# Six products into a residual, token-major instead of feature-major, in a two-block transformer kernel

## The chip, the core and the metric

The kernel runs on one core of a Trainium2 chip. The metric is the device time of one execution, in microseconds. Its engines, each with an instruction queue of its own: TensorE (PE, matmul), VectorE (DVE), ScalarE (ACT), GpSimd (POOL), SyncE (SP, which issues DMAs).

## The reference

Two blocks, of two layers each, over 256 latent tokens of width 1024 (the first block also carries 256 context tokens). Cut to what the change touches:

```
# first block, layer 1 (latents only)
h = h + ml[2] * (mix @ gdn_w_out)                                   # "dout"
h = h + ml[5] * (square(relu(modulate(rms_norm(h), ...) @ mlp_w1)) @ mlp_w2)   # "w2_1"
x = rms_norm(h, final_norm)
# second block, for l in (0, 1)
h = h + rms_norm(mixed @ w_out[l], norm_mix_post[l])                # "out0", "out1"
f = swiglu_ffn(rms_norm(h, norm_ffn_pre[l]), w_ffn_in[l], w_ffn_out[l])        # "fo0", "fo1"
h = h + rms_norm(f, norm_ffn_post[l])
```

All products are float32 in and out. `w_out` is 1024 x 1024, `mlp_w2` 4096 x 1024, `w_ffn_out` 2816 x 1024. Between the two layers of the second block the keys and values that layer 1 shares are made from the new h; the keys and values of a memory of 256 tokens are needed by both layers.

## The kernel before

The residual h lies feature-major: eight tiles of 128 features (partitions) x 256 tokens. A float32 product is three matmuls: both operands are split into a high part in the matmul's type and the remainder (hi and lo), and hi*hi, hi*lo and lo*hi are added up in PSUM. `load_w` fetches a weight tile of 128 x 1024 (512 KB) and splits it: ACT casts `whi` (L310), VectorE, or POOL where it is told to, subtracts for `wlo` (L311).

A product is feature-major: `gemm_fm` (L335 to L337) keeps 128x128 of the weights stationary and moves 256 tokens, for each of eight output tiles all its k tiles one after the other. `side_by_side` (L362 to L364) runs several output tiles k tile by k tile as activations arrive; most stretches begin with it, so L362 marks the first product behind a norm.

The norm's sum of squares of a token runs over the features, which are partitions. ACT squares each finished tile (L415, L418), POOL or VectorE adds the squares up (L419) while the next tile's product runs, TensorE adds the partitions with a column of ones (L398), VectorE takes x ** -0.5 by a polynomial (`newton`, L383 to L389: eight small dependent operations), and TensorE spreads the result over partitions (L408). In `post_norm` the norm falls on the product, so a copy of it, `mx`, waits for the factor: L1718 scales, L1719 adds to h, on VectorE for three tiles and on POOL for five. `fold` (L315, L316) then makes hi and lo of h times a weight for the next product, whose row factor is applied later, and `squares` (L1649, L1652) makes the next norm's squares.

Two lists of small work fill gaps: `fillers`, called by `fill`, and `sides`, called by `side`. In this part of the program the first holds `memory_prep` (memory tiles in hi and lo, with their norm), the second `memory_kv` (24 matmuls of 256 columns a step, with `mah`, `mal` for the memory, L335 to L337 or L345 to L347).

PSUM has two pools of four banks, `mm` and `sm`. The FFN (`ffn`) and the MLP (`mlp`) first make hidden tiles and then the output product; the MLP in four quarters of the hidden width, each adding to h (L759). The order of the engines' queues is set by a scheduler that works from the code's dependencies, the order the code calls in, and the pools.

Of the kernel before, what the change touches and what calls it, by code (L numbers as in the profile page):

```python
# [11 lines left out]
ALU = mybir.AluOpType  # L12
# [7 lines left out]
# x ** -0.5 = y * (p + P0) * (q + Q0) for a seed y with x * y * y within 0.93 .. 1.07, to 2.3e-8 of it  # L20
# [5 lines left out]
# ---------------------------------------------------------------- host layout  # L26
# [153 lines left out]
def _chunks_tm(w):  # L180
    """256 columns by half of K per block, for token-major products: [(N / 256) * 2, 128, 1024]"""
# [5 lines left out]
def host_arrays(i):  # L187
# [40 lines left out]
    ar["dout"] = _chunks(i["gdn_w_out"][0])  # L228
    for l in range(2):
# [3 lines left out]
        w = _chunks(i["w_ffn_out_2"][l])  # L233
        ar[f"fo{l}"] = np.ascontiguousarray(np.pad(w, ((0, 0), (0, 0), (0, 256))).reshape(8, 128, 3, 1024).transpose(0, 2, 1, 3))
# [6 lines left out]
    ar["out0"] = _chunks(i["w_out_2"][0])  # L241
    ar["out1"] = _chunks(i["w_out_2"][1][cat(order + [768 + al(256)])])
# [3 lines left out]
# ---------------------------------------------------------------- the kernel  # L246
# [3 lines left out]
class Kern:  # L250
# [12 lines left out]
    # ---- tiles  # L263
# [34 lines left out]
    def ftiles(self, n, name, R, dt=F32):  # L298
        """n feature tiles of [128, R]; two share a unit when R is 256"""
# [8 lines left out]
    # ---- building blocks  # L308
# [4 lines left out]
    def split_scaled(self, src, col, hi, lo):  # L313
        """hi + lo = src * col (per partition)"""
# [97 lines left out]
    def sq_acc(self, acc, src, first, eng):  # L412
        """acc += src ** 2"""
# [7 lines left out]
    def sq_accs(self, accs, src, f, eng, s=slice(0, 256)):  # L421
        """squares of the eight tiles of a norm, the last one's apart; s: the columns of src"""
# [4 lines left out]
    # ------------------------------------------------------------ program  # L427
# [4 lines left out]
    def body(self, es):  # L432
# [44 lines left out]
        acc = self.residual_out("dout", mix, 1, 2, 256, fills=2)  # L477
# [3 lines left out]
        acc = self.mlp(1, ah, al, 256, side_at=None)  # L481
# [24 lines left out]
    def ada_first(self, crow):  # L506
        """the first layer's shift and scale for each half of the feature tiles: on the tensor engine, but for the second half's scale"""
# [40 lines left out]
    def ada_cols(self, ps, out, bias):  # L548
        """rows of modulation vectors -> out, a column per feature tile, plus bias"""
# [28 lines left out]
    def side(self, n):  # L578
        """n steps of work on the tensor engine that only later parts wait for, where it would idle"""
# [8 lines left out]
    def fill(self, n):  # L588
        """up to n steps of work that other parts leave room for"""
# [8 lines left out]
    def by_turns(self, gens, turns):  # L598
        """the steps of several generators; turns: whose each one is, over and over"""
# [10 lines left out]
    def drain(self, n):  # L610
        """run the first n fillers to their end"""
# [7 lines left out]
    # ---- keys and values of the memory, both layers of the second block  # L619
    def memory_prep(self):  # L620
        """the memory in hi and lo parts, a feature tile per step, and its norm's factors"""
# [12 lines left out]
        y = self.rstd_cols([acc], 1024)  # L634
# [1056 lines left out]
    def post_norm(self, name, kt, weights, a, w, last=False, sides=(0, 0, 0), first=None, folds=()):  # L1691
# [24 lines left out]
        for f in range(8):  # L1716
# [6 lines left out]
            if False:  # L1723
                accs += self.squares([f], accs)
# [340 lines left out]
```

## Time and profile before

| | us |
|---|---|
| median of 3 runs | 1845.78 (1845.67 to 1847.97) |
| span of the profiled execution | 1845.4 |
| TensorE busy | 1750.0 (95%) |
| VectorE busy | 1320.7 (72%) |
| ACT busy | 824.8 (45%) |
| POOL busy | 372.2 (20%) |

The median lies 0.4 us above the span of the profiled execution. A busy share is an average over all stages. TensorE's 95% says little of a wait of some microseconds between two products: such waits are found in the engine's instructions in order of time, where the bracket behind an instruction gives the idle time ahead of it and what ended that. The granted clock is given per stretch, 1.00 being 2.4 GHz.

### The profile page before, as it was taken

Reading aid. Unit: us, or ns where it says so; the run is one execution under the profiler, and the core shown is the slowest. Engines: PE = TensorE matmul, PEld = TensorE weight load, DVE = VectorE, ACT = ScalarE, POOL = GpSimd, SP = SyncE. Lnnn points to the kernel's source line nnn. Section 1 sums busy time; section 2 is a strip of 40 time slices with the busy share of each in tenths; the row PEclk is TensorE's granted clock in tenths of the full one; section 3 lists DMA queues with packets and bytes.
Section 4 is the critical chain, followed back from the end, with each engine's and each line's share of the span. In section 5 each row is a group of like instructions: output and inputs, shape, how many; then the busy total and the mean of one; then the engine's idle time right before and its main releaser. Section 6 shows DMA issues by size and latency. Waiting matters only on the chain.

```text
span 1845.4 us, 31121 instructions
## 1 busy us (share of the span) xinstructions
PE 1750.0 (95%) x12076; PEld 1572.7 (85%) x12076; DVE 1320.7 (72%) x2443; ACT 824.8 (45%) x1476; POOL 372.2 (20%) x427
## 2 busy tenths in 40 slices
PE   8999999999999999888998999988999999999997
PEld 2786567888888889778997999987899998889997
DVE  6996787797957547689657766688777657677754
ACT  4433642532232336543334644556454435554442
POOL 1231131210201021136303000122211024231111
PEclk9999999899999999898798999999899999999999
DMA  8581001365747522235202555542455553145552
GB/s 316 161 273 58 23 18 57 102 216 172 246 166 245 172 93 88 64 103 151 57 25 80 182 182 185 180 146 69 150 190 184 174 184 126 47 140 185 184 174 85
DMA packets 99755, 260.82 MB, mean 141 GB/s; under 512 B 33492, under 2 KB 35412, under 8 KB 99352
## 3 DMA queue, kind: packets, MB, share of 16 engines
q1 hardware_dynamic: 99032, 257.47, 43.2%
q8 instruction: 95, 1.56, 0.3%
q10 hardware_dynamic: 576, 1.37, 0.2%
q14 instruction: 52, 0.43, 0.1%
HBM read 254.61 MB, written 4.19 MB: 140 GB/s over the span
## 4 chain that ended last, share of the span: by engine, by line
PE 71%; DVE 9%; ACT 2%; POOL 2%; issue 1%; DMA 0%; SPq 0%; POOLq 0%; ACTq 0%; DVEq 0%
PE mm L335 19%; PE mm L336 19%; PE mm L337 19%; PE mm L362 1%; PE mm L364 1%; PE mm L363 1%; DVE W L1393 1%; PE mm L1541 1%; DVE wlo L311 1%; PE mm L1532 1%; PE mm L1561 1%; PE sm L398 1%; DVE pr L1391 1%; PE sm L1578 1%; PE sm L1579 1%
## 5 line engine op out<-in xcount | busy, mean ns | idle before, releaser
L310 ACT CAST whi<-wst 128x1024 fp32r<-128x1024 f32 (+3 forms) x389 | 392.3, 1012 | 533.4 <-PE mm L336 288.1
L311 DVE TENSOR_TENSOR wlo<-wst,whi 128x1024 fp32r<-128x1024 f32 (+3 forms) x370 | 447.7, 1213 | 176.2 <-ACT whi L310 173.1
L335 PE MATMUL mm<-ah,whi 128*128 128x256 f32 (+1 forms) x1648 | 512.4, 313 | 3.7 <-DVE gs L1487 2.1
L336 PE MATMUL mm<-al,whi 128*128 128x256 f32 (+1 forms) x1648 | 513.4, 312 | 0.0
L337 PE MATMUL mm<-ah,wlo 128*128 128x256 f32 (+1 forms) x1648 | 512.5, 311 | 0.7 <-DVE wlo L311 0.7
L335 PEld LDWEIGHTS mm<-ah,whi 128*128 128x128 f32 x1648 | 316.7, 193 | 21.4 <-DVE gs L1487 2.5
L337 PEld LDWEIGHTS mm<-ah,wlo 128*128 128x128 f32 x1648 | 316.8, 192 | 17.2 <-DVE wlo L311 1.3
L336 PEld LDWEIGHTS mm<-al,whi 128*128 128x128 f32 x1648 | 317.1, 193 | 16.5 <-issue 0.8
L573 DVE SCALAR_TENSOR_TENSOR tmp<-adaw,crow 128x1024 bf16<-128x1024 f32 x134 | 162.1, 1236 | 4.3 <-DMA adaw<-in_ada 4.2
L335 PE MATMUL mm<-hh,whi 128*128 128x256 f32 (+1 forms) x480 | 159.7, 333 | 0.0
L336 PE MATMUL mm<-hl,whi 128*128 128x256 f32 (+1 forms) x480 | 159.6, 332 | 0.0
L337 PE MATMUL mm<-hh,wlo 128*128 128x256 f32 (+1 forms) x480 | 159.6, 332 | 0.0
L419 POOL TENSOR_TENSOR acc<-acc,tmp 128x256 f32<-128x256 f32 x57 | 63.1, 1117 | 435.0 <-ACT tmp L418 434.4
L575 POOL TENSOR_TENSOR mod<-mod,vecs 128x2 f32<-128x2 f32 (+1 forms) x84 | 62.7, 746 | 379.8 <-DVE tmp L573 339.2
L335 PE MATMUL mm<-fh,whi 128*128 128x256 f32 x352 | 99.6, 283 | 0.0
L336 PE MATMUL mm<-fl,whi 128*128 128x256 f32 x352 | 99.6, 283 | 0.0
L337 PE MATMUL mm<-fh,wlo 128*128 128x256 f32 x352 | 99.6, 283 | 0.0
L336 PEld LDWEIGHTS mm<-hl,whi 128*128 128x128 f32 x480 | 91.2, 190 | 8.8
L337 PEld LDWEIGHTS mm<-hh,wlo 128*128 128x128 f32 x480 | 91.2, 190 | 8.8
L335 PEld LDWEIGHTS mm<-hh,whi 128*128 128x128 f32 x480 | 91.2, 190 | 8.7
L759 DVE SCALAR_TENSOR_TENSOR h<-mm,mod,h 128x256 f32<-128x256 f32 x88 | 42.0, 481 | 68.5 <-PE mm L337 59.7
L335 PE MATMUL mm<-mh,whi 128*128 128x256 f32 (+1 forms) x240 | 76.3, 324 | 0.5 <-ACT whi L310 0.3
(471 smaller groups left out, 3312.0 us busy)
## 6 DMA issues: line engine op xcount, KB each, us to landing
wst<-in_w SPq DMA_DIRECT2D x128, 512.0 KB, 3.7
wst<-in_fin SPq DMA_DIRECT2D x88, 512.0 KB, 3.4
adaw<-in_ada SPq DMA_DIRECT2D x84, 512.0 KB, 4.3
wst<-in_fo SPq DMA_DIRECT2D x32, 512.0 KB, 3.4
wst<-in_dw SPq DMA_DIRECT2D x25, 512.0 KB, 3.3
wst<-in_out SPq DMA_DIRECT2D x16, 512.0 KB, 3.6
wst<-in_ew SPq DMA_DIRECT2D x14, 512.0 KB, 4.1
wst<-in_wa SPq DMA_DIRECT2D x14, 512.0 KB, 3.8
```

Source lines behind the costliest of these rows:

```text
L310: self.A.copy(hi, src)
L311: (lo_eng or self.V).tensor_tensor(lo, src, hi, ALU.subtract)
L335: T.matmul(out, lhsT=w[0][:, s], rhs=ah[k], start=(first and k == 0), stop=False)
L336: T.matmul(out, lhsT=w[0][:, s], rhs=al[k], start=False, stop=False)
L337: T.matmul(out, lhsT=w[1][:, s], rhs=ah[k], start=False, stop=(last and k == kt - 1))
L362: self.T.matmul(ps, lhsT=hi[:, s], rhs=ah[k], start=first and n == 0 and not (paired and i % 2), stop=False)
L363: self.T.matmul(ps, lhsT=lo[:, s], rhs=ah[k], start=False, stop=False)
L364: self.T.matmul(ps, lhsT=hi[:, s], rhs=al[k], start=False, stop=end)
L419: eng.tensor_tensor(acc, acc, s, ALU.add)
L573: V.scalar_tensor_tensor(self.tmp().bitcast(BF16), w, 0.5, crow[:, b], ALU.mult, ALU.mult, accum_out=m[:, b:b + 1])
L575: G.tensor_tensor(mm, mm, self.vec(f"adab{l}")[:, n:n + 1].to_broadcast([128, len(conds)]), ALU.add)
L759: self.V.scalar_tensor_tensor(h, ps[:, s], gt[:, f, b:b + 1], h, ALU.mult, ALU.add)
```

## The change

The six products become token-major, in a new class `Rows`. The activations are stationary (128 features of one k tile x 128 tokens), the weights move, 512 columns of a k tile's row block at a time. Four PSUM banks of the `sm` pool hold the result: two blocks of 128 tokens (tt) by two halves of the columns. `step` adds one k tile to all four banks as soon as its activations are made; the last three at most go token block by token block (`ends`), so that the first block is complete earlier. The MLP's hidden tiles go into the output product three tiles behind (`mlp_rows`), the FFN's likewise. The weights of the six products lie in DRAM as row blocks [k, 128, 1024]; tiles are as large and as many as before.

The norm of a product works on rows: ACT squares a bank and sums along it (L2124), VectorE adds the two sums (L2125) and runs `newton` on one column, VectorE and ACT scale the two banks by it (L2130, L2131), TensorE transposes the 1024 columns back, eight times 128x128 (L2097), VectorE adds to h with the weight (L2103). Where no norm falls on the product (`residual`, for dout and w2_1), banks are copied (L2110, L2111), transposed and added; the squares and their sums (L415 to L419) for the next norm start as h's tiles of the second token block are added. 2400 matmuls of 256 columns go, 1200 of 512 columns and 96 transposes come.

Further: `memory_prep` is spread over five k steps of dout, and its row factors take `mm` banks; attention in layer 1 takes two `mm` banks for its second group of outputs; `post_norm` calls one or two side steps, behind the second block's newton.

```diff
-        acc = self.residual_out("dout", mix, 1, 2, 256, fills=2)
+        rows = Rows(self, "dout", 8)
+        for k in range(5):
+            rows.step(k, mix[0][k], mix[1][k])
+            self.fill(2)
+        acc = rows.residual([(k, mix[0][k], mix[1][k]) for k in range(5, 8)], 1, 2)
...
-        acc = self.mlp(1, ah, al, 256, side_at=None)
+        acc = self.mlp_rows(1, ah, al)
...
+    def mlp_rows(self, l, ah, al):
...
+        lead = self.side_by_side([self.load_w(w1[f], G) for f in range(2)], 8, ah, al, 256)
+        for f in range(32):
...
+            A.activation(t, ps, AF.Relu)
+            V.tensor_mul(t2, t, t)
+            hid.append((f, *self.parts("hh")))
+            self.split(t2, *hid[-1][1:])
+            if len(hid) > 3:
+                rows.step(*hid.pop(0))
+        return rows.residual(hid, l, 5)
...
-        y = self.rstd_cols([acc], 1024)
+        y = self.rstd_cols([acc], 1024, cp=self.mm_ps())
...
+class Rows:
...
+    def add(self, w, ah, al, tt, half, first, last):
+        T, o = self.k.T, self.banks[tt][half]
+        ts, cs = slice(tt * 128, tt * 128 + 128), slice(half * 512, half * 512 + 512)
+        T.matmul(o, lhsT=ah[:, ts], rhs=w[0][:, cs], start=first, stop=False)
+        T.matmul(o, lhsT=al[:, ts], rhs=w[0][:, cs], start=False, stop=False)
+        T.matmul(o, lhsT=ah[:, ts], rhs=w[1][:, cs], start=False, stop=last)
...
+    def residual(self, left, l, gate):
+
+        k, gt, accs = self.k, self.k.mod(l, gate), []
+        for tt, banks in self.ends(left):
+            ys = k.units(2, "yt")
+            k.V.tensor_copy(ys[0], banks[0])
+            k.A.copy(ys[1], banks[1])
+            for f, p in self.columns(ys):
+                self.add_h(f, tt, p, gt[:, f, 0:1])
+                if tt:
+                    k.sq_accs(accs, k.h[:, f], f, k.G if f < 6 else k.V)
+        return accs
+
+    def normed(self, left, w, done, sides):
...
+        for tt, banks in self.ends(left):
+            sums, x = k.small(2, "nws"), k.small(32, "nwx")[:, 0:1]
+            for half in range(2):
+                k.A.activation(k.tmp(), banks[half], AF.Square, scale=1.0 / 32, accum_out=sums[:, half:half + 1])
+            k.V.scalar_tensor_tensor(x, sums[:, 0:1], EPS, sums[:, 1:2], ALU.add, ALU.add)
+            y = k.newton(x, 1)
+            if tt:
+                k.side(sides)
+            ys = k.units(2, "yt")
+            k.V.tensor_scalar(ys[0], banks[0], y, None, ALU.mult)
+            k.A.activation(ys[1], banks[1], AF.Copy, scale=y)
+            for f, p in self.columns(ys):
+                self.add_h(f, tt, p, w[:, f:f + 1])
+                done(tt, f)
```

POOL's queue around dout and the second MLP, before. The first `acc` row holds seven sums of the memory's squares and five of dout's, the next `acc` row w2's five; `wlo` are remainders of weight tiles, the pair those of the MLP's first two.

```order
L1424 TENSOR_TENSOR XT_8219<-Ca_8101,consts 128x512
L419 TENSOR_TENSOR acc<-acc,tmp 128x256 x12
L311 TENSOR_TENSOR wlo<-wst,whi 128x1024 x2
L419 TENSOR_TENSOR acc<-acc,tmp 128x256 x5
L311 TENSOR_TENSOR wlo<-wst,whi 128x1024
```

After the change:

```order
L1454 TENSOR_TENSOR XT_8219<-Ca_8101,consts 128x512
L419 TENSOR_TENSOR acc<-acc,tmp 128x256 x7
L311 TENSOR_TENSOR wlo<-wst,whi 128x1024 x2
L419 TENSOR_TENSOR acc<-acc,tmp 128x256 x5
L311 TENSOR_TENSOR wlo<-wst,whi 128x1024
L419 TENSOR_TENSOR acc<-acc,tmp 128x256 x5
```

The pair of weight remainders stood behind dout's five sums and stands ahead of them; the row of five behind it is dout's, the next w2's.

VectorE's queue between the end of out0 and the first addition to h, before: `newton` is L383 to L389, `mkT` a memory key, `mx` the product that waits for the norm.

```order
L311 TENSOR_TENSOR wlo<-wst,whi 128x1024
L646 TENSOR_TENSOR mkT_9062<-mm,mbc 128x256
L400 TENSOR_SCALAR nwx<-sm 128x2
L383 TENSOR_SCALAR nwy<-nwx 128x2
L384 SCALAR_TENSOR_TENSOR nwt<-nwy 128x2
L311 TENSOR_TENSOR wlo<-wst,whi 128x1024
L385 TENSOR_TENSOR nwt<-nwt,nwx 128x2
L386 SCALAR_TENSOR_TENSOR nwp<-nwt 128x2
L387 SCALAR_TENSOR_TENSOR nwt<-nwt 128x2
L388 SCALAR_TENSOR_TENSOR nwp<-nwp,nwy 128x2
L389 SCALAR_TENSOR_TENSOR nwy<-nwt,nwp 128x2
L1718 SCALAR_TENSOR_TENSOR mx_12715<-mx_12715,vecs,sm 128x256 x2
```

After the change, the second token block's newton up to its scaled rows `yt`:

```order
L383 TENSOR_SCALAR nwy<-nwx 128x1
L650 TENSOR_TENSOR mkT_9053<-mm,mbc 128x256
L384 SCALAR_TENSOR_TENSOR nwt<-nwy 128x1
L311 TENSOR_TENSOR wlo<-wst,whi 128x1024
L385 TENSOR_TENSOR nwt<-nwt,nwx 128x1
L311 TENSOR_TENSOR wlo<-wst,whi 128x1024
L386 SCALAR_TENSOR_TENSOR nwp<-nwt 128x1
L311 TENSOR_TENSOR wlo<-wst,whi 128x1024
L387 SCALAR_TENSOR_TENSOR nwt<-nwt 128x1
L388 SCALAR_TENSOR_TENSOR nwp<-nwp,nwy 128x1
L389 SCALAR_TENSOR_TENSOR nwy<-nwt,nwp 128x1
L2130 TENSOR_SCALAR yt_12498<-sm,nwy 128x512
```

One weight remainder stood between the newton's steps; three and the memory key stand there now.

## Rows read from the trace of the kernel before

**Rows 1.** The last-ended chain on the page: share of the span by engine.

```profile
PE 71%; DVE 9%; ACT 2%; POOL 2%; issue 1%; DMA 0%; SPq 0%; POOLq 0%; ACTq 0%; DVEq 0%
```

**Rows 2.** Busy by stretch: start:end, length, PE, PEld, DVE, ACT, POOL (instructions), PEclk, DMA, GB/s.

```profile
1030.00:1190.00 160.00, 160.00 (x1336) 160.00 (x1335) 102.25 (x142) 76.35 (x117) 1.16 (x1) 1.00 0.57 184
400.00:660.00 260.00, 260.00 (x1149) 215.29 (x1148) 184.22 (x279) 79.10 (x98) 30.99 (x49) 1.00 0.62 202
```

**Rows 3.** TensorE in order of time: start, length, then [idle before <-what ended it], dout.

```profile
980.11 0.97 PE L335 MATMUL mm<-mh,whi 128*128 128x256 f32 x4
...
997.98 0.37 PE L398 MATMUL sm<-ones,acc 128*128 128x1 f32 x1 [2.98 <-POOL acc L419]
...
1011.26 0.35 PE L398 MATMUL sm<-ones,acc 128*128 128x1 f32 x2 [0.47 <-DVE acc L419]
...
1018.87 0.28 PE L362 MATMUL mm<-ah,whi 128*128 128x256 f32 x1
```

**Rows 4.** Busy time by stretch, columns as in rows 2: behind that stall.

```profile
998.00:1005.00 7.00, 7.00 (x34) 7.00 (x35) 4.21 (x10) 2.21 (x3) 1.14 (x1) 0.53 0.39 126
```

**Rows 5.** TensorE in order of time, w2 to the next product.

```profile
1204.37 0.35 PE L398 MATMUL sm<-ones,acc 128*128 128x1 f32 x2 [1.02 <-DVE acc L419]
...
1213.05 0.39 PE L362 MATMUL mm<-ah,whi 128*128 128x256 f32 x1 [1.36 <-ACT ah L315]
```

**Rows 6.** TensorE in order of time, out0 to the first FFN.

```profile
1309.97 0.28 PE L335 MATMUL mm<-mah,whi 128*128 128x256 f32 x1
...
1319.40 0.58 PE L362 MATMUL mm<-ah,whi 128*128 128x256 f32 x1 [1.84 <-ACT ah L315]
```

**Rows 7.** TensorE in order of time, fo0 to the shared keys.

```profile
1514.69 0.28 PE L335 MATMUL mm<-mah,whi 128*128 128x256 f32 x1
...
1529.65 0.39 PE L362 MATMUL mm<-ah,whi 128*128 128x256 f32 x1
```

**Rows 8.** TensorE in order of time, out1 to the second FFN.

```profile
1631.11 0.32 PE L398 MATMUL sm<-ones,acc 128*128 128x1 f32 x2
...
1637.51 0.58 PE L362 MATMUL mm<-ah,whi 128*128 128x256 f32 x1 [1.84 <-ACT ah L315]
```

**Rows 9.** TensorE and POOL in order of time, the end.

```profile
1832.45 0.28 PE L398 MATMUL sm<-ones,acc 128*128 128x1 f32 x2
...
1835.97 0.68 PE L408 MATMUL sm<-consts,nwy 128*128 128x128 f32 x4 [1.60 <-DVE nwy L389]
...
1839.09 3.56 POOL L1719 TENSOR_TENSOR h<-h,mx 128x256 f32<-128x256 f32 x5 [19.46 <-DVE mx L1718]
```

**Rows 10.** Groups by line: total us, mean ns of one | idle before.

```profile
L311 DVE TENSOR_TENSOR wlo<-wst,whi 128x1024 fp32r<-128x1024 f32 (+3 forms) x370 | 447.7, 1213 | 176.2 <-ACT whi L310 173.1
...
L419 POOL TENSOR_TENSOR acc<-acc,tmp 128x256 f32<-128x256 f32 x57 | 63.1, 1117 | 435.0 <-ACT tmp L418 434.4
...
L966 ACT ACTIVATE p<-mm,nm 128x512 f32<-128x512 f32 x16 | 10.9, 684 | 13.7 <-DVE nm L962 13.7
...
L966 ACT ACTIVATION_READ_ACCUMULATOR p<-mm,nm 128x1 f32 x32 | 6.6, 205 | 0.0
...
L985 ACT COPY pT<-sm 128x512 f32<-128x512 f32 x16 | 8.8, 604 | 2.3 <-PE sm L983 2.3
...
L1567 DVE SCALAR_TENSOR_TENSOR S<-S,ge,mm 128x128 f32<-128x128 f32 x48 | 13.2, 343 | 6.4 <-PE mm L1561 6.4
...
L418 ACT ACTIVATE tmp<-h 128x256 f32<-128x256 f32 x31 | 12.1, 409 | 7.7 <-DVE nwy L389 4.0 <-DVE nwy L383 2.9 <-DVE h L759 0.8
```

**Rows 11.** POOL and VectorE in order of time, beside each other behind fo0.

```profile
1515.94 2.39 POOL L311 TENSOR_TENSOR wlo<-wst,whi 128x1024 fp32r<-128x1024 f32 x1 [14.07 <-ACT whi L310]
...
1517.77 0.42 DVE L646 TENSOR_TENSOR mkT<-mm,mbc 128x256 f32<-128x256 f32 x1 [2.45 <-PE mm L337]
...
1518.82 2.38 POOL L311 TENSOR_TENSOR wlo<-wst,whi 128x1024 fp32r<-128x1024 f32 x1 [0.49 <-ACT whi L310]
...
1518.96 2.25 DVE L384 SCALAR_TENSOR_TENSOR nwt<-nwy 128x2 f32<-128x2 f32 x1
```

More of the change, by code (lines that the diff above doesn't have):

```diff
@@ L223, in host_arrays @@
         ar[f"w1_{l}"] = _chunks(i["mlp_w1"][l])
-        ar[f"w2_{l}"] = cat([_chunks(i["mlp_w2"][l][q * 1024:(q + 1) * 1024]) for q in range(4)], 0)
+    ar["w2_0"] = cat([_chunks(i["mlp_w2"][0][q * 1024:(q + 1) * 1024]) for q in range(4)], 0)
+    ar["w2_1"] = i["mlp_w2"][1].reshape(32, 128, 1024)
     w = i["gdn_w_in"][0]
@@ L240, in host_arrays @@
     ar["wb"] = _chunks(i["w_in_b_2"][0], cat(order + [768 + al(256)]))
-    ar["out0"] = _chunks(i["w_out_2"][0])
-    ar["out1"] = _chunks(i["w_out_2"][1][cat(order + [768 + al(256)])])
+    ar["out0"] = i["w_out_2"][0].reshape(8, 128, 1024)
+    ar["out1"] = i["w_out_2"][1][cat(order + [768 + al(256)])].reshape(8, 128, 1024)
     return ar
@@ L1673, in second_block @@
         self.side(0)
-        acc, a = self.post_norm("out0", 8, lambda f: [(self.aps["out0"][f], 8)], mix, "mpost0", sides=(1, 0, 0), first=first, folds=("fpre0",))
+        acc, a = self.post_norm(first, [(k, mix[0][k], mix[1][k]) for k in range(6)], "mpost0", folds=("fpre0",), sides=1)
         self.dump("hb0", [self.h[:, f] for f in range(8)])
@@ L1678, in second_block @@
         mix, first = self.swa_mixer(a, bc, kv)
-        acc, a = self.post_norm("out1", 8, lambda f: [(self.aps["out1"][f], 8)], mix, "mpost1", first=first, folds=("fpre1",))
+        acc, a = self.post_norm(first, [(k, mix[0][k], mix[1][k]) for k in range(3, 6)], "mpost1", folds=("fpre1",))
         self.dump("hb1", [self.h[:, f] for f in range(8)])
         self.ffn(1, acc, a, ())
-    def lead_out(self, name, n, ks, mh, ml):
-        ws = [self.load_w(self.aps[name][f]) for f in range(n)]
-        banks = [self.mm_ps() for _ in range((n + 1) // 2)]
-        out = [banks[f // 2][:, (f % 2) * 256:(f % 2) * 256 + 256] for f in range(n)]
-        self.k_tiles(ws, ks, mh, ml, out, True, False, True)
-        return ws, out, [k for k in range(8) if k not in ks]
@@ new lines, in post_norm, with done @@
+    def post_norm(self, rows, left, w, last=False, folds=(), sides=0):
+        fs = self.folds(*folds)
+        def done(tt, f):
+            s = slice(tt * 128, tt * 128 + 128)
+            if last:
+                if f % 2:
+                    self.S.dma_start(self.aps["out"].rearrange("p (f t) -> p f t", f=8)[:, f - 1:f + 1, s], self.h[:, f - 1:f + 1, s])
+            else:
+                self.fold(fs[:1], f, s)
+        rows.normed(left, self.vec(w), done, sides)
+        if last:
+            return
+        accs = self.squares()
@@ L1755, in ffn @@
             G.tensor_tensor(u, u, g, ALU.mult)
-            self.split(u, fh[f], fl[f])
-        return self.post_norm(f"fo{l}", 22, lambda f: [(self.aps[f"fo{l}"][f, k][:, :n * 128], n) for k, n in enumerate((8, 8, 6))],
-                              (fh, fl), f"fpost{l}", last=l == 1, sides=(1, 0, 9), folds=folds)
+            hid.append((f, *self.parts("fh")))
+            self.split(u, *hid[-1][1:])
+            if len(hid) > 3:
+                rows.step(*hid.pop(0))
+        return self.post_norm(rows, hid, f"fpost{l}", last=l == 1, folds=folds, sides=2 * (l == 0))
     def lru_mixer(self, a, accs):
@@ L1848, in lru_mixer @@
             elif c == "L":
-                first = self.lead_out("out0", 1, (6, 7), mh, ml)
+                first = Rows(self, "out0", 8)
+                for n in (6, 7):
+                    first.step(n, mh[n], ml[n])
             else:
@@ L2035, in swa_mixer @@
                 if qt == 0:
-                    po[tg] = [self.sm_ps(), self.sm_ps()]
+                    po[tg] = [(self.mm_ps if tg else self.sm_ps)() for _ in range(2)]
                 outputs(tg, qt)
@@ L2041, in swa_mixer @@
             elif c == "L":
-                first = self.lead_out("out1", 3, (6, 7, 0, 1, 2), mh, ml)
+                first = Rows(self, "out1", 8)
+                for n in (6, 7, 0, 1, 2):
+                    first.step(n, mh[n], ml[n])
             else:
```

101 lines of the change are left out of this document (54 added, 47 removed).

## Prediction

> **What bounds the kernel now.** I read the page's last-ended chain first: TensorE carries 71% of it, VectorE 9% [rows 1]. So matmul work counts at its full price wherever TensorE never waits, and elsewhere it is the path between two products that counts. The second view, busy time by stretch, tells these apart: 1030 to 1190 us, the second MLP, is busy for all of its 160 us at clock 1.00 [rows 2]. The third, TensorE's instructions in order of time at the six places where a product ends and a norm stands before the next product, gives the length of each such seam [rows 3, 5 to 9]. There the row to look for is the first matmul of the next product (L362), and in brackets what it waited for. The groups by line [rows 10] give the price of one operation each.
>
> **The loops.** The change replaces two 256-column matmuls by one of 512 columns. In 1030 to 1190, 1336 matmuls, all of 256 columns, fill 160 us: 119.8 ns each. In 400 to 660, 1149 matmuls, of 512 columns, fill 260 us: 226.3 ns each [rows 2]. A pair so saves 2 x 119.8 - 226.3 = 13.3 ns. The second MLP's output product has 32 k tiles x 4 banks x 3 terms = 384 long matmuls: 5.1 us; each FFN's 22 x 12 = 264: 3.5 us; each of the three projections' 96: 1.3 us. MLP and FFNs together save 12.1 us. I count them in full, since the loops stay TensorE's. One step of the new MLP loop is 24 short and 12 long matmuls, 24 x 0.120 + 12 x 0.226 = 5.6 us; beside it VectorE makes two weight remainders, 2 x 1.21 [rows 10], and ACT as many casts as before. The projections' savings come with their seams.
>
> By the Trainium skill, page "TensorE: Matmul & The Clock Gate", section "Back-to-back issue gap", an isolated matmul takes N/2.4 + 2.5 ns, 109.2 and 215.8 ns. By that a pair saves 2.5 ns, and 1200 pairs 3.0 us instead of 15.9. The traced spacings lie some 11 to 13 ns above its figures, so the sum goes by the trace.
>
> **The seams.** Token-major sums of a row can't be completed while products still run, so each norm starts after the last product: copy of two banks, 0.60 (L985 [rows 10]); four transposes, not shown in the trace as a stretch of their own, between nothing and 4 x 0.12 (a 256-column matmul's spacing), taken at 0.48; additions to the residual of 128x128, 0.34 each (L1567 [rows 10]). The eight transposes of the first token block stand between products: 8 x 0.12 = 0.96 us at every seam.
>
> *dout to the second MLP.* Before: products from 980.11, a 2.98 us stall on the memory's sums at 997.98, accumulators ready at 1011.26 (31.2 us), first MLP matmul 7.6 later [rows 3]. After the stall the clock is low: 34 matmuls in 7.00 us at 0.53 [rows 4] instead of 34 x 0.12 = 4.1, so a wait like this costs 2.9 more. The change spreads the memory's sums over five k steps and puts its factors into the other PSUM pool. The products now take 96 x 0.226 = 21.7, transposes 0.96, and I leave some 2 for waits: T1, the last product, at 24.7 instead of 31.2, -6.5. Behind T1, now: copy and transposes 1.1. Meanwhile POOL, in whose queue the first two w1 remainders stand ahead of the five sums of this norm (before, behind them), makes them for 2 x 2.4 [rows 11]; with their casts just ahead of the copy they start about 1.0 before T1 and end 3.8 after it. Five sums of 1.12 [rows 10]: 9.4. VectorE's own sum and the row sums: 10.2. Newton, which before took 1.60 [rows 9] alone, has one remainder (1.21) and two memory keys (0.42 each [rows 11]) between its steps: 13.8. Broadcast 0.7 [rows 9] and the first tile's three operations, at the square's 0.41 and a little more, 1.4: 15.9 instead of 7.6, +8.3. The 48 memory matmuls that covered this wait before cover now only its first 5.8, then TensorE idles and, as after the earlier stall, loses 2.9. Sum -6.5 + 8.3 + 2.9 = +4.7. Ends: -1 if the POOL work is done in time and the clock stays up, +9 if the products save nothing.
>
> Whether POOL's remainders also stop VectorE decides part of it. In the trace a newton step (two SBUF inputs) that begins with such a remainder takes 2.25, to its end; a product with one PSUM input beside another takes 0.42 [rows 11]. So the additions to h, which read PSUM, pass, and the remainders on VectorE would not. The Trainium skill, page "GPSIMD Engine Reference", section "1. Specifications", has the same, contention with two SBUF inputs; held additions too would by those rows add up to 2.2 us here.
>
> *w2 to the final norm.* Before, the last product ends 1.02 ahead of 1204.37, the next product starts 1213.05: 9.7 [rows 5], as the squares ran beside the products, a tile at a time. Now copy, transposes, first addition and square come first, 0.60 + 0.48 + 0.34 + 0.41 [rows 10] = 1.8, then five POOL sums of 1.12 and VectorE's, 0.5: row sums 7.9 after T1; from there as before, 8.7. 16.6 - 9.7 + 0.96 = +7.9. Ends: +4 (POOL uncontended), +11 (with a low clock).
>
> *out0 to the first FFN.* Before 1319.40 - 1309.97 = 9.4 [rows 6], with side matmuls in it. Now: the square of a bank with its sum read, 0.68 + 0.21 [rows 10], behind up to three ACT casts, so 0.9 to 3.7; newton 1.6 with three weight remainders and memory keys inside, 3 x 1.21 + 0.42 = 4.1; scaled copy 0.60, transposes 0.48, addition 0.34, first folded tile 0.5 (an estimate from the square's 0.41): 8.5 to 11.3. With 0.96 - 1.27 for product and transposes: -1.2 to +1.6, and the remainders may come before the newton or later: -2 to +3. Taken +1.0, near the upper sum, since ACT's casts do stand ahead.
>
> *fo0 to the shared keys.* Before 1529.65 - 1514.69 = 15.0 [rows 7], two chained feature-major passes over h with POOL additions. Now square 0.9, newton and two remainders 4.0, copy and transposes 1.1, eight additions 2.7, the next norm's eight squares 3.3 and two chained sums 1.0: 13.0, plus 0.96: -1.0 (-4 to +1).
>
> *out1 to the second FFN.* Before 6.4 [rows 8]. Now square 0.9, newton 1.6, remainders 1.2 to 2.4, copy, transposes, addition, fold 1.9, casts ahead 1 to 2: 6.6 to 8.8, TensorE idle throughout, and 0.96 - 1.27: 0 to +2; a low clock 0 to 2.9 more. Taken +1.8 (-1 to +4).
>
> *fo1, the end.* Before: last product 1832.6, h complete 1842.65, end 1845.4 [rows 9]: 12.8. Now square 0.9, sum and newton 1.8, copy and transposes 1.1, additions 8 x 0.34 = 2.7, and the last landing 2.75 as before: 9.2, plus 0.96: 10.2. -2.6, taken -3.0, as the squares of the first bank run early (-5 to -2).
>
> **Sum.** -12.1 + 4.7 + 7.9 + 1.0 - 1.0 + 1.8 - 3.0 = -0.7. The profiled execution spans 1845.4, the runs' median is 1845.78, 0.4 above: 1845.1 forecast for the median. Nearly all that TensorE saves is given back where norms now wait for whole rows.
>
> **Rivals.**
> A, faster: the seams are shorter. For it: POOL's remainders may be done before T1, the VectorE remainders inside the newton run in time that it would wait anyway, and squares are off POOL in four seams. Against: the queue orders, which put them there whatever the time. dout 0, w2 +4, out0 -1, fo0 -2, out1 0, fo1 -4: -15.1, 1831; with half of this 1838.
> B, slower: one mechanism, the low clock behind an exposed norm. TensorE has no side work left at w2, out0, fo0 and out1, idles 6 to 12 us in each, and starts the next product at the lower of its two levels (1.2 of 2.4 GHz), 2.9 us each by rows 4. For it: those rows. Against: the waits of before at 1213.05 and 1319.40 [rows 5, 6] left loops that are full at 1.00 soon after. All four: +11.6, 1857; from two on (+5.8) the kernel is slower.
> C: the change doesn't do what it says, since a long matmul costs here as much as two short ones, or the row steps come late and stop the loop. Against the first: rows 2; against the second: the 5.6 us step, of which VectorE fills some 3.3. All 15.9 lost: 1861. By the Trainium skill's rule above 12.9 would be lost: 1858; the trace disagrees by its spacings.
>
> **How the numbers follow.** Forecast with its own range 1839 to 1851: 0.48. A 0.25, B 0.22, C 0.05. What this kernel's measurement can tell from no change is about 0.2%, 3.7 us: 1842.1 to 1849.5. Of the forecast's share 0.14 lies below, 0.24 within, 0.10 above; A gives 0.25 below; B 0.18 above and 0.04 within; C 0.05 above. Faster 0.39, same 0.28, slower 0.33. The range, 1834 to 1856, leaves out the outer parts of A, B and C.
>
> **What would show it.** MLP and FFN loops at about 5.1 and 3.5 us less each; at dout T1 at about 24 us behind the first product, and then L362 waiting for some 10 us on VectorE or ACT, with POOL's L419 sums behind two L311 of 2.4; at w2 the wait for L398 on POOL or VectorE grown by 6 to 7 us; at the end 10 us instead of 12.8 behind the last product. The forecast is wrong if POOL's sums run at T1 without a remainder ahead (then A), or if the granted clock reads 0.5 behind more than one of the other seams (then B).

## The result, and the profile after

1857.35 us, median of 4 runs (1856.04 to 1857.68), against 1845.72: ratio 1.0059 (95% interval 1.0047 to 1.0071). The change makes the kernel 0.6% slower; the time lies 1.4 us above the range of the prediction and is that of its rival B, 1857, though, as the traces and runs below show, only in small part for B's reason. The profiled execution took 1857.57 us and spans 1855.5, 10.1 more than the one before.

The chain on the page, which answers to [rows 1]:

```profile
PE 37%; DVE 5%; issue 2%; ACT 2%; POOL 0%; DVEq 0%; ACTq 0%; POOLq 0%
```

Its sum is 46% instead of 85, so it was followed back over a shorter part of the span; what can be compared is the stretch. Busy time by stretch of the changed kernel, columns as in [rows 2]: a full stretch of the new MLP loop, and the first 96 matmuls behind dout's norm.

```profile
1050.00:1190.00 140.00, 140.00 (x898) 127.74 (x897) 78.08 (x100) 66.67 (x101) 0.00 (x0) 1.00 0.58 188
1027.30:1040.90 13.60, 13.60 (x96) 13.60 (x97) 8.26 (x19) 9.59 (x22) 0.00 (x0) 0.83 0.18 60
```

The loop is as forecast: always busy, full clock, 898 matmuls in 140 us, 36 of them (24 short, 12 long) in 5.61 us. The long matmul pays. The second line is the start of the MLP at 0.83: 13.6 us for what takes 11.5 at full clock.

A seam, below, is the time from the start of the last matmul of a product to the first L362 behind it. TensorE, POOL and VectorE in order of time at dout, after the change (to be read beside [rows 3]):

```profile
1007.94 0.39 PE L2067 MATMUL sm<-wlo,mh 128*128 128x512 f32 x1
...
1008.85 4.87 POOL L311 TENSOR_TENSOR wlo<-wst,whi 128x1024 fp32r<-128x1024 f32 x2 [11.07 <-ACT whi L310]
...
1013.66 3.95 POOL L419 TENSOR_TENSOR acc<-acc,tmp 128x256 f32<-128x256 f32 x5
...
1018.12 0.42 PE L398 MATMUL sm<-ones,acc 128*128 128x1 f32 x2 [4.79 <-DVE acc L419]
...
1020.06 0.17 DVE L383 TENSOR_SCALAR nwy<-nwx 128x2 int32<-128x2 int32 x1
...
1023.27 0.42 DVE L650 TENSOR_TENSOR mkT<-mm,mbc 128x256 f32<-128x256 f32 x1 [1.45 <-PE mm L337]
...
1023.87 0.16 DVE L389 SCALAR_TENSOR_TENSOR nwy<-nwt,nwp 128x2 f32<-128x2 f32 x1
...
1027.30 0.58 PE L362 MATMUL mm<-ah,whi 128*128 128x256 f32 x1 [1.99 <-ACT ah L310]
```

The two weight remainders run behind the last product, not before it, and the five sums behind them. Counted from the start of the last matmul, the row sums (L398) start at 10.2 us, the newton's first step (L383) at 12.1, its last step ends at 16.1, and the next product starts at 19.4 (before: 8.4). The memory key L650 stands between two steps of the newton and waits 1.45 us for memory products of TensorE. The last part is no longer than before, where the broadcast of the factor starts 3.4 us ahead of the next product (1018.87 [rows 3]):

```profile
1015.48 0.68 PE L408 MATMUL sm<-consts,nwy 128*128 128x128 f32 x4 [0.21 <-DVE nwy L389]
```

At w2_1, answering to [rows 5], TensorE of the changed kernel:

```profile
1210.36 0.40 PE L2067 MATMUL sm<-wlo,hh 128*128 128x512 f32 x1
...
1219.22 0.38 PE L398 MATMUL sm<-ones,acc 128*128 128x1 f32 x2 [3.43 <-DVE acc L419]
...
1227.23 0.58 PE L362 MATMUL mm<-ah,whi 128*128 128x256 f32 x1 [2.30 <-ACT ah L315]
```

At out0, answering to [rows 6], all engines, the rows of the path only: ACT's folds of the first token block, the square of the second block's last bank, the newton's steps on VectorE and what stands between them.

```profile
1323.78 0.39 PE L2067 MATMUL sm<-wlo,mh 128*128 128x512 f32 x1
...
1324.97 1.29 ACT L315 ACTIVATE ah<-h,vecs 128x128 fp32r<-128x128 f32 x4
...
1326.15 0.59 ACT L2124 ACTIVATE tmp<-sm 128x512 f32<-128x512 f32 x1
...
1326.94 1.22 DVE L311 TENSOR_TENSOR wlo<-wst,whi 128x1024 fp32r<-128x1024 f32 x1
...
1328.83 1.22 DVE L311 TENSOR_TENSOR wlo<-wst,whi 128x1024 fp32r<-128x1024 f32 x1
...
1330.04 1.22 DVE L311 TENSOR_TENSOR wlo<-wst,whi 128x1024 fp32r<-128x1024 f32 x1
...
1331.24 1.22 DVE L311 TENSOR_TENSOR wlo<-wst,whi 128x1024 fp32r<-128x1024 f32 x1
...
1332.63 0.16 DVE L389 SCALAR_TENSOR_TENSOR nwy<-nwt,nwp 128x1 f32<-128x1 f32 x1
...
1335.63 0.58 PE L362 MATMUL mm<-ah,whi 128*128 128x256 f32 x1
```

The square starts 2.1 us behind the last product, since ACT first casts and folds for the first block. Four remainders, 4.9 us, then stand in and ahead of a newton of eight steps. The same picture at out1, where TensorE has nothing else to do:

```profile
1652.85 1.97 PE L2097 MATMUL sm<-consts,yt 128*128 128x128 f32 x8 [8.32 <-DVE yt L2130]
...
1654.84 0.58 PE L362 MATMUL mm<-ah,whi 128*128 128x256 f32 x1
```

At fo0 POOL and VectorE run side by side, answering to [rows 11]:

```profile
1531.66 4.94 POOL L311 TENSOR_TENSOR wlo<-wst,whi 128x1024 fp32r<-128x1024 f32 x2 [14.43 <-ACT whi L310]
...
1531.92 2.47 DVE L316 SCALAR_TENSOR_TENSOR al<-h,vecs,ah 128x128 fp32r<-128x128 f32 x1
...
1534.71 1.92 DVE L384 SCALAR_TENSOR_TENSOR nwt<-nwy 128x1 f32<-128x1 f32 x1
```

Two operations of 0.35 and 0.16 us last until POOL's remainder beside each ends: 3.9 us in VectorE's queue. But the next product waits here for more than the newton, which ends at 1538.5. Behind the last product TensorE makes 72 products for the memory's keys and values, and one of them waits for the remainder of its own weights, which VectorE makes behind the held step. All engines, in order of time:

```profile
1536.55 1.21 DVE L311 TENSOR_TENSOR wlo<-wst,whi 128x1024 fp32r<-128x1024 f32 x1
...
1537.82 0.58 PE L347 MATMUL mm<-wlo,mah 128*128 128x256 f32 x1 [2.66 <-DVE wlo L311]
...
1542.75 1.04 ACT L310 CAST whi<-wst 128x1024 fp32r<-128x1024 f32 x1 [6.82 <-PE mm L346]
...
1544.42 0.69 ACT L2131 ACTIVATE yt<-sm,nwy 128x512 f32<-128x512 f32 x1
...
1545.16 0.66 PE L2097 MATMUL sm<-consts,yt 128*128 128x128 f32 x4 [1.43 <-ACT yt L2131]
```

The 72 products take 14.9 us (1527.83 to 1542.68), where 72 x 0.12 would be 8.6. ACT scales the second bank only behind a cast that waits for them, and L362 starts at 1545.80. And the end, answering to [rows 9]:

```profile
1846.05 0.39 PE L2067 MATMUL sm<-wlo,fh 128*128 128x512 f32 x1
...
1848.62 0.75 DVE L2130 TENSOR_SCALAR yt<-sm,nwy 128x512 f32<-128x512 f32 x1
...
1850.12 2.16 DVE L2103 SCALAR_TENSOR_TENSOR h<-sm,vecs,h 128x128 f32<-128x128 f32 x8 [0.75 <-PE sm L2097]
```

From the last product to the end of the span 9.5 us, instead of 13.1.

The spans differ by 10.1 us; the table in the section on the prediction gives where.

A part of it lies ahead of dout, which starts 2.4 us later (982.48 instead of 980.11), and isn't the change's: up to there TensorE's work is the same, 5512 matmuls in the first 976 us of either trace. Busy time by stretch before the change, then after it:

```profile
924.00:932.00 8.00, 7.93 (x88) 7.28 (x85) 5.96 (x21) 4.01 (x12) 0.00 (x0) 1.00 0.00 0
```

```profile
924.00:932.00 8.00, 7.93 (x97) 7.25 (x95) 4.20 (x17) 3.47 (x9) 0.00 (x0) 0.79 0.01 2
```

The clock fell in the same work in one execution and not in the other. In the fourteen profiled executions dout starts between 978.3 and 983.3.

### The profile page after: what moved, and what is told of

The parts are those of the page before. It is cut to its first block, busy times and chain, and to the rows that moved or that the text cites. A ratio compares the mean times of both kernels' runs of the same rounds, so it can differ in the third digit from the quotient of the medians.

```text
span 1855.5 us, 28652 instructions
## 1 busy us (share of the span) xinstructions
PE 1748.9 (94%) x10924; PEld 1517.5 (82%) x10924; DVE 1304.5 (70%) x2483; ACT 834.1 (45%) x1508; POOL 323.1 (17%) x387
## 5 line engine op out<-in xcount | busy, mean ns | idle before, releaser
L310 ACT CAST whi<-wst 128x1024 fp32r<-128x1024 f32 (+2 forms) x385 | 391.9, 1021 | 562.3 <-PE mm L336 227.4
L311 DVE TENSOR_TENSOR wlo<-wst,whi 128x1024 fp32r<-128x1024 f32 (+2 forms) x366 | 445.6, 1220 | 208.6 <-ACT whi L310 206.7
L337 PEld LDWEIGHTS mm<-ah,wlo 128*128 128x128 f32 x1648 | 316.3, 192 | 16.9 <-DVE wlo L311 1.2
L335 PE MATMUL mm<-hh,whi 128*128 128x512 f32 (+1 forms) x288 | 105.4, 366 | 0.0
L337 PE MATMUL mm<-hh,wlo 128*128 128x512 f32 (+1 forms) x288 | 105.2, 365 | 0.0
L336 PE MATMUL mm<-hl,whi 128*128 128x512 f32 (+1 forms) x288 | 105.2, 365 | 0.0
L311 POOL TENSOR_TENSOR wlo<-wst,whi 128x1024 fp32r<-128x1024 f32 x19 | 46.6, 2460 | 269.9 <-ACT whi L310 243.4
L2066 PE MATMUL sm<-whi,fh 128*128 128x512 f32 x176 | 69.1, 393 | 0.0
L2065 PE MATMUL sm<-whi,fh 128*128 128x512 f32 x176 | 69.0, 392 | 0.0
L2067 PE MATMUL sm<-wlo,fh 128*128 128x512 f32 x176 | 68.5, 389 | 0.0
L335 PEld LDWEIGHTS mm<-hh,whi 128*128 128x128 f32 x288 | 54.3, 189 | 8.8
L337 PEld LDWEIGHTS mm<-hh,wlo 128*128 128x128 f32 x288 | 54.3, 189 | 8.8
```

The costliest lines, as they stand in the source:

```text
L310: self.A.copy(hi, src)
L311: (lo_eng or self.V).tensor_tensor(lo, src, hi, ALU.subtract)
L335: T.matmul(out, lhsT=w[0][:, s], rhs=ah[k], start=(first and k == 0), stop=False)
L336: T.matmul(out, lhsT=w[0][:, s], rhs=al[k], start=False, stop=False)
L337: T.matmul(out, lhsT=w[1][:, s], rhs=ah[k], start=False, stop=(last and k == kt - 1))
L2065: T.matmul(o, lhsT=ah[:, ts], rhs=w[0][:, cs], start=first, stop=False)
```

## The experiments

One table of seams first, start of the last matmul to the first L362, in us, from the trace of each kernel; behind it the ratio to the kernel before with its interval.

| kernel | dout | w2_1 | out0 | fo0 | out1 | median us | ratio |
|---|---|---|---|---|---|---|---|
| before | 8.4 | 10.0 | 9.5 | 15.1 | 6.5 | 1845.7 | |
| after | 19.4 | 16.9 | 11.9 | 18.2 | 10.7 | 1857.4 | 1.0059 (1.0047 to 1.0071) |
| e1 second block only | 8.4 | 10.0 | 11.8 | 16.3 | 10.7 | 1840.0 | 0.9965 (0.9952 to 0.9977) |
| e2 fo0 and fo1 only | 8.4 | 10.0 | 9.5 | 17.6 | 7.0 | 1840.9 | 0.9970 (0.9959 to 0.9980) |
| e3 fo1 only | 8.4 | 10.0 | 9.5 | 15.1 | 6.5 | 1839.7 | 0.9965 (0.9952 to 0.9978) |
| e4 POOL out of dout, w2_1 | 16.1 | 13.3 | 11.8 | 17.4 | 10.7 | 1847.0 | 1.0003 (0.9992 to 1.0015) |
| f4 remainders off POOL | 17.5 | 17.3 | 11.8 | 18.2 | 10.7 | 1852.9 | 1.0039 (1.0024 to 1.0054) |
| f1 e4, remainders behind newton | 12.4 | 13.3 | 9.8 | 17.6 | 9.7 | 1842.9 | 0.9979 (0.9970 to 0.9989) |
| f2 e4, folds late | 16.1 | 13.3 | 9.8 | 13.0 | 8.6 | 1841.3 | 0.9976 (0.9966 to 0.9985) |
| f12 both | 12.4 | 13.3 | 6.7 | 13.0 | 7.5 | 1833.1 | 0.9923 (0.9905 to 0.9942) |
| h1 after, clock kept up | 20.4 | 18.8 | 11.4 | 17.6 | 10.2 | 1853.5 | 1.0034 (1.0022 to 1.0047) |
| h2 f12, fo0 off POOL | 12.4 | 13.3 | 6.7 | 12.1 | 7.5 | 1831.0 | 0.9914 (0.9893 to 0.9934) |
| h3 f12, dout feature-major | 7.5 | 13.3 | 6.7 | 13.0 | 7.5 | 1835.7 | 0.9942 (0.9923 to 0.9960) |
| h4 h2, clock kept up | 12.2 | 13.9 | 6.7 | 12.1 | 6.4 | 1834.9 | 0.9939 (0.9924 to 0.9954) |

**Which products cost.**

```diff
+        acc = self.residual_out("dout", mix, 1, 2, 256, fills=2)
-        acc = self.mlp_rows(1, ah, al)
+        acc = self.mlp(1, ah, al, 256, side_at=None)
```

> dout and w2_1 feature-major again, as before the change; the four products of the second block token-major. Theory (the loss is what stands behind the last product of dout and of w2_1: 19.1 and 16.6 us instead of 7.6 and 9.9, and about 2 us of low clock behind each; the second block gains 4 us in the trace, 6.6 without that low clock): about 1839 to 1842. Rival (each norm that waits for whole rows costs what its product saves, in either block alike): 1846 to 1849.

1840.0: the theory's range. The first block's two products cost what made the change slow.

e2 and e3 keep the kernel before and put only fo0 and fo1, or fo1 alone, into rows:

```diff
-            self.split(u, fh[f], fl[f])
...
+            hid.append((f, *self.parts("fh")))
+            self.split(u, *hid[-1][1:])
+            if len(hid) > 3:
+                rows.step(*hid.pop(0))
```

> Only the output products of the two FFNs (fo0, fo1) token-major. Theory: the second FFN's loop gives 3.5 us and the end behind it 3.7, the first FFN's loop 3.1, its seam takes some 1.5 to 3 back: 1836 to 1839. Rival (fo0's seam with POOL's weight remainders takes more than its loop gives): 1840 to 1843.

> Only fo1 token-major. Theory: loop -3.5 and end -3.7, all else as before: 1838 to 1839. Rival (the loop's gain is partly waits that move): 1841 to 1843. With the run of both FFN products, it tells whether fo0 gains (theory: 0 to 3 us) or loses.

1840.9, the rival's range, and 1839.7, between the two. In e3's trace the loop gives 2.1 us and the end 3.7, the one product without a norm that another waits for. fo0 adds nothing that these intervals can tell: in e2's trace its loop gives 2.0, its seam takes 2.5, and the stretch from there to out1's end gives 1.5.

**POOL's part.**

```diff
-                    k.sq_accs(accs, k.h[:, f], f, k.G if f < 6 else k.V)
+                    k.sq_accs(accs, k.h[:, f], f, k.V)
...
-        lead = self.side_by_side([self.load_w(w1[f], G) for f in range(2)], 8, ah, al, 256)
+        lead = self.side_by_side([self.load_w(w1[f]) for f in range(2)], 8, ah, al, 256)
```

> The changed kernel with POOL taken out of the norms behind dout and w2_1: all eight sums of squares and the MLP's first two weight remainders on VectorE. Theory (POOL's 4.9 us of remainders and 3.95 us of sums are the path behind dout, its sums the path behind w2_1): row sums some 3.5 us earlier at dout, 2 at w2_1, of which the remainders, now in VectorE's queue, take up to 2.4 back: 1852 to 1854. Rival (the newton and the low clock set it; VectorE only takes the wait over): 1857.

1847.0, 10 us below the changed kernel where 3 to 5 were expected. The spans differ by 8.7: 3.2 and 3.6 at the two seams (expected about 1.5 and 2), 0.8 at fo0, and 1.3 ahead of dout, which is none of its doing. f4 has the second edit alone:

```diff
-        lead = self.side_by_side([self.load_w(w1[f], G) for f in range(2)], 8, ah, al, 256)
+        lead = self.side_by_side([self.load_w(w1[f]) for f in range(2)], 8, ah, al, 256)
```

> The changed kernel (1857.4) with one of the two edits of e4 alone: the MLP's first two weight remainders on VectorE, the sums of squares still on POOL. Theory (both stand in the path behind dout, only the sums in the one behind w2_1): dout's row sums start 2.8 us sooner, VectorE's queue takes up to 2.4 back, w2_1's seam stays: 1853 to 1856. Rival (the remainders are all of what e4 won, 10 us): 1847 to 1849.

1852.9, the lower end of the theory's range, by 1.8 us at dout's seam and none at w2_1's. So at dout the remainders ahead of the sums and the sums themselves each count; at w2_1 it is the sums, which stand in POOL's queue behind another remainder, of 2.5 us, that neither edit moves. What was left at dout, in e4 (TensorE and VectorE, the newton's wait):

```profile
1015.07 1.21 DVE L311 TENSOR_TENSOR wlo<-wst,whi 128x1024 fp32r<-128x1024 f32 x1
...
1016.27 1.22 DVE L311 TENSOR_TENSOR wlo<-wst,whi 128x1024 fp32r<-128x1024 f32 x1
...
1017.47 1.22 DVE L311 TENSOR_TENSOR wlo<-wst,whi 128x1024 fp32r<-128x1024 f32 x1
...
1019.47 0.58 PE L408 MATMUL sm<-consts,nwy 128*128 128x128 f32 x1 [4.52 <-DVE nwy L389]
```

Three remainders of the next product's weights stand ahead of or between the steps of a newton that takes no more than 1.6 us alone [rows 9].

**What stands in the newton, and ahead of it.** f1 queues the next weights' remainders on VectorE behind the newton's last step:

```diff
             if tt:
                 k.side(sides)
+                k.hold = [k.last_newton.ins]
```

(the same line in `norm_mod` and `final_norm`; `load_w` orders VectorE's remainder behind what `hold` names).

> e4 (1847.0) with the next product's weight remainders queued on VectorE behind the newton, instead of between its eight steps, at dout, w2_1, out0, fo0 and out1. Theory (the remainders lengthen the newton by 2.4 us at dout, 3.6 at out0 and out1, 1.2 at fo0, and only the first tile's 1.2 is wanted soon behind it): 1839 to 1842. Rival (the next product waits for these remainders as long as for the norm): 1845 to 1847.

f2 folds once, behind the second block:

```diff
-            else:
-                self.fold(fs[:1], f, s)
+            elif tt:
+                self.fold(fs[:1], f)
```

> e4 (1847.0) with the fold of h for the next product made once over 256 tokens behind the second token block, not per block: ACT's casts and folds of the first block no longer stand ahead of the second block's squares, which started 2.1 us behind the last product at out0, 2.0 at out1. Theory: 2 us each at out0 and out1, 1 to 2 at fo0, of which the longer folds behind the norm take about 0.3 each back: 1842 to 1844. Rival (VectorE's remainders fill the newton whenever it starts): 1846 to 1847.

> e4 with both edits, remainders behind the newton and folds behind the second block. Theory (two separate terms of the same path, so they add): 1835 to 1839. Rival (either alone uncovers the same third wait, ACT's cast of the next tile): no better than the better of the two.

1842.9, 1841.3 and 1833.1. f1 comes out a microsecond above the theory's range by its time, f2 and f12 0.7 and 1.9 below theirs. f1's seams are 3.7 shorter at dout, 2.0 at out0, 1.0 at out1. f2 takes 2.0 at out0, 4.3 at fo0, 2.1 at out1. At fo0 POOL holds VectorE in f2 as long as before, a remainder for 3.37 us instead of 1.2 and a newton step for 2.36 instead of 0.16; what is gone there is the late start of the newton, by 1.9, and the waits of the 72 memory products, which take 8.6 us instead of e4's 14.0. Both together take 3.2 at out1, the sum of the two, and 5.1 at out0, a microsecond more than the sum: two terms of one path. VectorE's newton in f1 at dout, then in f12 at out0:

```profile
1012.01 0.17 DVE L383 TENSOR_SCALAR nwy<-nwx 128x2 int32<-128x2 int32 x1
...
1013.34 0.16 DVE L389 SCALAR_TENSOR_TENSOR nwy<-nwt,nwp 128x2 f32<-128x2 f32 x1
1013.41 1.22 DVE L311 TENSOR_TENSOR wlo<-wst,whi 128x1024 fp32r<-128x1024 f32 x1
```

```profile
1310.74 0.15 DVE L383 TENSOR_SCALAR nwy<-nwx 128x1 int32<-128x1 int32 x1
...
1311.78 0.16 DVE L389 SCALAR_TENSOR_TENSOR nwy<-nwt,nwp 128x1 f32<-128x1 f32 x1
```

1.3 and 1.0 us from the first step to the last, where the changed kernel's out0 has 4.3 (1328.37 to 1332.63). f12 is the change with its queues mended: 0.8% faster than before.

**The low clock.** h1 gives TensorE unread products where the changed kernel idles:

```diff
+    def warm(self, n, a):
+        ps = self.mm_ps()[:, :256]
+        for i in range(n):
+            self.T.matmul(ps, lhsT=a[:, 0:128], rhs=a, start=True, stop=True)
```

> The changed kernel (1857.4) with products that nobody reads on TensorE where it idled behind the last product: 36 of 256 columns at dout (4.3 us of work where it idled 5.1), 24 at w2_1 (2.9 of 3.7), 48 at out0 (5.8 of 6.9), 64 at out1 (7.7 of 8.7). No wait of another engine changes. Theory (a low clock behind these waits is a cost of its own: 2.0 us in the first 96 matmuls behind dout, 2.7 in the first 50 behind w2_1, about 1.5 each at out0 and out1): 1849 to 1852. Rival (the low clock lies where TensorE waits anyway): 1856 to 1858.

1853.5, between the two, its interval touching that of the changed kernel: not settled by time. The clock did stay up behind dout (busy time by stretch, h1, the first 99 matmuls):

```profile
1029.30:1040.80 11.50, 11.50 (x99) 11.50 (x97) 10.34 (x21) 10.14 (x22) 0.00 (x0) 1.00 0.41 134
```

From one product's end to the next h1 gains 1.1 us at dout, 1.9 at out0 and 1.1 at out1, and loses 1.9 at w2_1 and 0.9 at fo0; the trace is that of the slowest of its six runs, 1857.69, and its span is no shorter than the changed kernel's. So where it was kept up, the clock gave 1 to 2 us a seam in this trace, less than the 2.9 of rival B, and unread products give it back at most in part.

**What is left.**

```diff
-        lead = self.side_by_side([self.load_w(self.aps["sk"][t], self.G) for t in range(2)], 8, *a, 256)
+        lead = self.side_by_side([self.load_w(self.aps["sk"][t]) for t in range(2)], 8, *a, 256)
```

> f12_both (1833.1) with the two weight remainders of the shared keys, which run on POOL during the newton behind fo0, on VectorE. In f12's trace a VectorE remainder beside them takes 3.37 instead of 1.2 us and one newton step 2.35 instead of 0.16: 4.3 us held. Theory (POOL's remainders hold VectorE): those 4.3 go, 2.4 come for the remainders, which are now queued behind the newton: 1829 to 1832. Rival (TensorE's memory products set this seam): 1833.

1831.0, in the theory's range; but the interval overlaps f12's, and fo0's seam is 0.9 shorter, not 2. The held steps are gone, the newton ends 4.4 us sooner behind the last product than in f12, and three remainders follow it ahead of the scaled rows. VectorE, and ACT's cast that waits for the memory products:

```profile
1514.55 3.68 DVE L311 TENSOR_TENSOR wlo<-wst,whi 128x1024 fp32r<-128x1024 f32 x3
1518.15 0.74 DVE L2135 TENSOR_SCALAR yt<-sm,nwy 128x512 f32<-128x512 f32 x1
...
1518.80 1.05 ACT L310 CAST whi<-wst 128x1024 fp32r<-128x1024 f32 x1 [1.83 <-PE mm L346]
```

TensorE is busy with the 72 memory products until 1518.7, and transposes the first bank at 1518.95; ACT's scaled copy of the second bank comes at 1520.48, behind that cast. So by this trace the rival's cause, the memory products, is the next bound of the seam. No run tests that; an order behind the scaled copy, which wasn't tried, would move the three remainders but not these products.

```diff
-        rows = Rows(self, "dout", 8)
...
+        acc = self.residual_out("dout", mix, 1, 2, 256, fills=2)
```

> f12_both (1833.1) with dout alone feature-major again, and the memory's sums as before the change. Theory (with the queues mended dout's row form is worth nothing: products 5.5 us shorter, norm behind them some 7 longer, low clock included): 1831 to 1834. Rival (dout's row form now pays, since the 2.98 us stall and the low clock behind it come back here): 1836 to 1838.

1835.7, between the two expectations, and overlapping f12. From dout's first matmul to the MLP's first: 38.8 us before, 44.8 after, 37.8 in f12, 37.1 in h3. With the queues mended, rows are worth nothing at dout that these runs can tell; what helps is the mended queue.

h4 takes h2 with h1's products, fewer of them:

```diff
+        k.warm({"dout": 8, "w2_1": 8}[self.name], last)
...
+                n = {'out0': 8, 'out1': 32}.get(self.name, 0)
```

> f12_both with the edit of h2 and unread products in what idle time is left: 8 at dout, w2_1 and out0, 32 at out1 (3.8 of 4.5 us). Theory (terms add): 2 from h2, 2 to 3 from the clock: 1827 to 1831. Rival (the unread products delay what waits behind them): above h2.

1834.9, not below h2: the rival. out1's seam is 1.1 shorter, w2_1's 0.6 longer, and the time shows no gain.

## Why the prediction was wrong

Its views and its loops held; its seams, w2_1's apart, were sized too small, and at fo0 the path was another. By its own terms, the first block's eight transposes counted with the stretch they lie in, from the two traces (us, after less before):

| stretch | forecast | measured |
|---|---|---|
| ahead of dout | 0 | +2.4 |
| dout's product | -6.5 | -4.9 |
| dout's seam | +8.3 | +11.0 |
| MLP loop, with the low clock at its start | -1.2 | -1.1 |
| w2_1's seam | +6.9 | +6.9 |
| up to out0's end | -0.3 | -0.3 |
| out0's seam | +1.3 | +2.3 |
| first FFN | -2.5 | -3.2 |
| fo0's seam | -2.0 | +3.1 |
| up to out1's end | -0.3 | -3.0 |
| out1's seam | +2.1 | +4.2 |
| second FFN | -2.5 | -3.6 |
| end | -4.0 | -3.6 |
| sum | -0.7 | +10.1 |

- **Loops and w2_1**: right in size. The step of 5.6 us is 5.61; e4 wins 3.6 at w2_1 by taking the sums off POOL. The exact +6.9 there is partly luck: the row sums start 8.9 us behind the last matmul, not 7.9, with another remainder ahead of the sums on POOL, and the rest takes 8.0, not 8.7.
- **dout's seam**: the order of POOL's queue was read rightly, and the sums are done about when reckoned, though by two errors that cancel: "they start about 1.0 before T1" failed, the remainders start 0.9 behind the start of the last matmul, and the five sums take 3.95, not 5.6. Two steps failed behind that. "VectorE's own sum and the row sums: 10.2" is where the row sums only start; the newton begins at 12.1. And the broadcast with the first tile's three operations, 0.7 and 1.4, takes 3.3 from the newton's end; the kernel before already had 3.4 there. The newton itself takes 4.0, near the 3.6 reckoned, though by other terms: one of the two memory keys stands in it and waits 1.45 for its products on TensorE, at low clock. A memory product that was to cover the wait lengthens it.
- **fo0's seam**, the largest miss: "newton and two remainders 4.0" failed, it is 7.8 from the sum of the squares (1530.68) to the newton's end, since POOL's remainders beside it held VectorE for 3.9. [rows 11] show that at this very place in the kernel before, and it was weighed at dout alone. The second failure is the path: the sum of 13.0 follows the norm, and the 72 memory products on TensorE, with ACT's work behind them, have no term in it. They end 4.2 us behind the newton. f2's 13.0 is the forecast's length by another path, with VectorE held as long; with the hold gone, in h2, the seam is 12.1.
- **Up to out1's end**, 2.7 better than the sum had it, is the other side of fo0. The kernel before starts its next product early and then waits, at a lower clock; the changed one starts late and doesn't stop. Busy time by stretch, the first 10 us from L362 on, before and after:

```profile
1529.65:1539.65 10.00, 8.13 (x55) 7.93 (x54) 7.84 (x17) 8.27 (x20) 2.67 (x4) 0.83 0.17 52
1545.80:1555.80 10.00, 10.00 (x85) 10.00 (x85) 8.21 (x26) 9.54 (x25) 1.59 (x2) 1.00 0.16 54
```

  30 matmuls more, some 3.6 us of work at 0.12 each. The two rows of the table together were forecast at -2.3 and came to +0.1.
- **out0 and out1**: "three weight remainders" were four at out0 and "remainders 1.2 to 2.4" three, 3.7, at out1; the squares start 2 us late at both, which the sums had allowed for. The transposes ahead of L362 take 1.97 for eight, at low clock, twice the 0.48 that was counted for four. f1 takes out the remainders, f2 the late squares.
- "The runs' median is 1845.78, 0.4 above" the span was a wrong bridge: a run of the changed kernel takes 2.1 more than its span (1857.57 and 1855.5), and the runs of the kernel before that were taken beside the experiments 1.7 to 1.8 more than theirs. So its profiled execution, of span 1845.4, took about 1847.2, 1.4 above its median: that is the difference between +10.1 in the spans and +11.6 in the medians.

Rival B had the sum, 1857, by luck. It priced the low clock at 2.9 us in each of w2_1, out0, fo0 and out1. Busy time by stretch from L362 on, before and after, at w2_1 and then at out0:

```profile
1213.05:1216.85 3.80, 3.80 (x30) 3.75 (x31) 3.80 (x10) 3.80 (x11) 1.17 (x2) 1.00 0.68 254
1227.23:1231.03 3.80, 3.80 (x18) 3.80 (x19) 3.77 (x11) 3.47 (x10) 0.73 (x1) 0.50 0.94 316
1319.40:1323.80 4.40, 4.40 (x20) 4.40 (x21) 4.11 (x10) 3.41 (x9) 2.62 (x4) 0.50 0.00 0
1335.63:1340.03 4.40, 4.40 (x23) 4.40 (x24) 4.17 (x15) 4.40 (x15) 1.23 (x2) 0.60 0.22 88
```

The clock is low behind out0, and behind out1, in the kernel before too. The first 60 matmuls of 256 columns from L362 on take 2.1 us more than before at dout and 2.5 more at w2_1, and less than before at out0, fo0 and out1 (11.2, 9.1 and 10.5 against 11.6, 12.2 and 11.4). So of B's four places the low clock is new at w2_1 alone, 2.5 us; at dout, where the forecast has 2.9 for it, it is 2.1. The larger part was work of other queues in the path: e4, f1 and f2 together take 24 us off, with TensorE's work unchanged. Rival A's -15 is near what f12 reaches, -13, once that work is moved. Rival C is out, since the long matmul pays in every loop. By the Trainium skill, page "TensorE: Matmul & The Clock Gate", section "Back-to-back issue gap", an isolated matmul takes N/2.4 + 2.5 ns; an estimate from that for the loop's step is 24 x 0.109 + 12 x 0.216 = 5.2 us. The trace has 5.61.

## What to carry to other kernels

A product that is cheaper on its engine can lose it all where its norm stops being made tile by tile beside the product: work out the path from the last matmul to the next one, engine by engine, before counting the loop. Then look what the scheduler has put into that path: weight preparation for the next product, ready early and needed late, slips between the small steps of a norm, and an order edge or a later fold takes it out again. A product whose result nobody on the chip waits for, like the last one, is the place where such a change pays by itself.

## What the runs showed of the hardware

- VectorE operations with two SBUF inputs that start beside POOL's 128x1024 remainder: 0.35 and 0.16 us became 2.47 and 1.92, while a memory key with one PSUM input between them kept its 0.41; in f12's trace two POOL remainders took 5.92 instead of 4.87 beside a VectorE one. The Trainium skill, "GPSIMD Engine Reference", section "1. Specifications", names such contention. The price here is the whole rest of the other's operation.
- Kernels with the same work of TensorE up to dout reach it at 978.3 to 983.3 us, as TensorE's clock falls in some of the same short waits and not in others. A term of 2 us can't be read from two traces.
